# The down-projection of a hybrid decoder layer as seven block products: weight sums formed during FoX attention, zero blocks on ScalarE, low parts and additions on VectorE

## The chip, the cores and the metric

The kernel runs on one core of a Trainium2 chip. The metric is the device time of one execution in microseconds, the median of several runs. Engine names follow the profile: PE is TensorE (PEld its weight loads), DVE is VectorE, ACT is ScalarE, POOL is GpSimd, and SP is SyncE, which here only issues transfers.

## The reference

One decoder layer on 2048 tokens of width 1024, all in float32. The part that matters here:

```python
h = rms_norm(x, g_attn[l]) * (1.0 + scale_a) + shift_a
proj = h @ w_in[l]                      # FoX q|k|v, stick-breaking q|k|v, forget gates
o_fox = forgetting_attention(...)       # 8 heads of 64, causal softmax with a forget bias
o_sb = stick_breaking_attention(...)    # 8 heads of 64
x = x + gate_a * (mix @ w_out[l])

h = rms_norm(x, g_mlp[l]) * (1.0 + scale_m) + shift_m
u = causal_depthwise_conv(h @ w_up[l], conv_w[l], conv_b[l])
u_gate, u_val = jnp.split(u, 2, axis=-1)            # each 2752 wide
x = x + gate_m * ((jax.nn.silu(u_gate) * u_val) @ w_down[l])
return rms_norm(x, g_final)
```

`shift`, `scale` and `gate` come from a conditioning vector through `w_ada` (adaLN). The down-projection is the last product: 2048 tokens by 2752 by 1024.

## The kernel before

Every float32 operand of a matmul is split by `split` into a high part (a ScalarE copy, rounded to TensorE's fast float32 format) and a low part (the difference, by GpSimd unless VectorE is named). A product is then three matmuls: high by high, high by low, low by high.

The program has five stages: the stick-breaking heads with their input projections, the FoX heads with theirs, the output projection with the second norm, the up-projection with convolution and gating, and the down-projection with the final norm. In the attention stages a unit is a pair of heads and a block of 512 queries (4 pairs x 4 blocks for each kind). `interleave` runs a unit's attention and, in between, steps of generators: the projections of the next unit, and in FoX units the generator `late_mod` (4 steps a unit), which computes the rest of the adaLN modulation, folds `gate_a` into `w_out` (`fold_out`) and, at the end of its gate part, stores `gate_m` to device memory (line 565). Projection inputs and everything of `late_mod` live in one pool of ten tiles named `hp`. In `weighted`, a diagonal block's upper quarter of the tile `at` is zeroed by GpSimd (line 391) before ScalarE writes the rest. `Fd` (line 446) is the causal mask that GpSimd writes into the forget bias.

The up-projection already works as seven block products in place of eight (Winograd's form of Strassen's scheme): `h_operands` and `w_operands` form sums of quarter blocks, `pair` runs the products. It starts each half of the tokens with `h_operands`, whose tiles are `oa` and `ob`.

The down-projection runs plainly: for each of four blocks of 512 tokens, 22 row blocks of `w_down` (the last half full) are loaded and split each time, and eight banks of PSUM accumulate all of them. The last four row blocks are kept back so that the banks finish one after the other; then the gate, the residual `x1s`, the final norm and the store follow.

The program's code gives each engine a list of instructions in order; the scheduler of the framework places them by its own timeline, so that neighbouring stages overlap a little. Each engine works through its list in that order, and SP issues its transfers in that order too.

Of the kernel before, what the change touches and what calls it, by code (L numbers as in the profile page):

```python
# [33 lines left out]
def kernel(ctx: ExitStack, tc: tile.TileContext, x, c, w_ada, b_ada, g_attn, w_in, b_fgate,  # L34
# [28 lines left out]
    gate_m = dram.tile([P, D], F32, name="gate_m")  # L63
# [318 lines left out]
    def weighted(o, kts, blk, V, hl, first, last, diag):  # L382
# [7 lines left out]
        if diag:  # L390
            nc.gpsimd.memset(f(at[:, :, 0:P]), 0.0)
# [132 lines left out]

    def late_mod():
# [15 lines left out]
        for part, gate in late:  # L541
# [12 lines left out]
            if gate is not None:  # L554
# [7 lines left out]
                if gate == 0:  # L562
                    yield from fold_out(gt)
                else:
                    nc.sync.dma_start(gate_m, gt)
# [93 lines left out]
    for i, u in enumerate(units):  # L659
# [20 lines left out]
        if nxt is None:  # L680
# [10 lines left out]
                    (lm if kind == "fox" and (p, tb) != (0, 0) else None, 4, False), (tail, 12, True)])  # L691
# [44 lines left out]

    ho1 = open_pool("hop1")
# [12 lines left out]
    def h_operands(sblk, j):  # L750

        pool = ho if j == 0 else ho1
# [3 lines left out]
        b = pool.tile([P, 3, 2, TB], F32R, name=f"ob{j}")  # L756
        a = pool.tile([P, 4, 2, TB], F32R, name=f"oa{j}")
# [5 lines left out]
        def put(hi, lo, s, lo_engine=None):  # L763
            split(hi, lo, s, lo_engine or nc.vector)
# [8 lines left out]
        put(a[:, 1:3, 0], a[:, 1:3, 1], xh[:, 1].rearrange("p (a n) -> p a n", n=TB), nc.gpsimd)  # L773
# [150 lines left out]
    close_pool("up", "hop1", "wup", "hop0")  # L924

    dp = open_pool("down", side="right")

    def load(k, tb):
        n = P if k < NFULL else REST
        g = dp.tile([P, 2, TB], F32R, name="g", bufs=6)  # L930
        wraw = dp.tile([P, D], F32, name="wdraw", bufs=3)
        graw = dp.tile([P, TB], F32, name="graw", bufs=2)
        w = dp.tile([P, 2, D], F32R, name="wd", bufs=6)
        for r in range(P // n):
            nc.sync.dma_start(wraw[r * n:(r + 1) * n], w_down[k * P:k * P + n, :])
            nc.sync.dma_start(graw[r * n:(r + 1) * n], gs[k][tb // 2][:, tb % 2 * TB:(tb % 2 + 1) * TB])
        split(w[:, 0], w[:, 1], wraw, nc.vector)
        if n == P:
            split(g[:, 0], g[:, 1], graw)
        else:  # L940
            nc.scalar.activation(g[:, 0], graw, AF.Copy)
            nc.vector.tensor_sub(g[REST:P, 0], graw[REST:P], f(g[REST:P, 0]))
        return g, w

    de = open_pool("end")
    gm = de.tile([P, D], F32, name="gm")
# [3 lines left out]
    for tb in range(NTB):  # L950
# [13 lines left out]
        for k in range(NKD):  # L964
            g, w = load(k, tb)
            if k >= NKD - LAST:
                tail.append((k, g, w))
                continue
# [52 lines left out]
```

## Time and profile before

| | us |
|---|---|
| median of 3 runs (3137.22 to 3140.04) | 3139.62 |
| the profiled execution | 3137.58 |
| its span, first to last instruction | 3135.8 |
| TensorE busy | 2962.9 |
| VectorE busy | 2142.5 |
| ScalarE busy | 1650.2 |
| GpSimd busy | 1281.3 |

The page's busy times overlap, since the engines work side by side; a matmul's own duration also overlaps its neighbour's, so the pace of matmuls is taken from stretches of them. A row of a group reads: line, engine, operation, tile written, tiles read, shapes and count, then busy time and mean ns of one, then idle time before them and who ended it. A row of the waits reads: who waited, for whom, us in total, times, longest.

### The profile page before, as it was taken

To read this page: it belongs to the slowest core of one execution; us is meant where nothing else is said; L and a number is where in the kernel's file an instruction comes from. 1 tells how busy PE (TensorE), PEld (TensorE's weight loads), DVE (VectorE), ACT (ScalarE), POOL (GpSimd) and SP (SyncE) were. 2 spreads that over 40 slices of the span, in tenths; PEclk is the share of its full clock that TensorE was granted. 3 is DMA by queue.
4 is the path that set the end of the run, shared out by engine and by line. 5 is a ranking of instruction groups with operands and counts; after the bars stand their busy time and mean duration, and the time that the engine had idled before them with its cause. 6 is when DMAs were issued, how large, how long until landed. Compare 5 with 4: busy or idle time off the path is not lost. (4 is left out here: it accounts for less than half of the span.)

```text
span 3135.8 us, 46430 instructions
## 1 busy us (share of the span) xinstructions
PE 2962.9 (94%) x15934; PEld 2508.4 (80%) x15934; DVE 2142.5 (68%) x3334; ACT 1650.2 (53%) x3033; POOL 1281.3 (41%) x1523
## 2 busy tenths in 40 slices
PE   6889998999989999999999899999899998999998
PEld 5778787878878888888877688888678887888887
DVE  6787988888866765557832677778887776254253
ACT  5665666666656665567733444444444444333332
POOL 2564455456553343352212444444544442332321
PEclk8999999999999999999999999999999999999999
DMA  9447642556346796595456532223222223554552
GB/s 268 170 149 250 175 139 64 189 178 167 124 150 184 258 279 209 152 328 137 161 186 220 195 98 81 81 81 88 77 89 86 81 81 137 186 199 161 188 200 89
DMA packets 292940, 496.51 MB, mean 158 GB/s; under 512 B 29448, under 2 KB 177664, under 8 KB 291680
## 3 DMA queue, kind: packets, MB, share of 16 engines
q1 hardware_dynamic: 281072, 480.92, 48.0%
q10 hardware_dynamic: 11632, 12.63, 1.1%
q8 instruction: 126, 2.06, 0.3%
q14 instruction: 110, 0.90, 0.1%
HBM read 352.61 MB, written 90.51 MB: 141 GB/s over the span
## 5 line engine op out<-in xcount | busy, mean ns | idle before, releaser
L810 PE MATMUL ps_o<-oa,wu 128*128 128x512 f32 x2088 | 506.2, 393 | 18.1 <-DVE oa L45 12.0
L810 PEld LDWEIGHTS ps_o<-oa,wu 128*128 128x128 f32 x2088 | 392.4, 189 | 110.0 <-DVE oa L45 15.7
L397 PE MATMUL ps_pv<-at,V 128*128 128x256 f32 x2304 | 404.7, 294 | 36.2 <-DVE at L393 19.5
L393 DVE TENSOR_TENSOR at<-ps_pt,at 128x512 fp32r<-128x512 f32 (+1 forms) x576 | 364.0, 652 | 107.2 <-ACT at L392 104.2
L281 PE MATMUL ps_pj<-hp,w_qk 128*128 128x512 f32 x1512 | 415.2, 405 | 14.2 <-DMA hp<-hs 4.4
L392 ACT ACTIVATE at<-ps_pt 128x512 fp32r<-128x512 f32 (+1 forms) x576 | 314.4, 576 | 210.2 <-PE ps_pt L388 161.0
L420 POOL TENSOR_TENSOR a<-a,r 128x512 f32<-128x512 f32 (+3 forms) x240 | 286.8, 1196 | 309.8 <-DVE r L419 88.5
L397 PEld LDWEIGHTS ps_pv<-at,V 128*128 128x128 f32 x2304 | 334.6, 191 | 81.0 <-DVE at L393 34.5
L281 PEld LDWEIGHTS ps_pj<-hp,w_qk 128*128 128x128 f32 x1512 | 275.6, 191 | 68.7 <-DMA hp<-hs 6.9
L45 DVE TENSOR_TENSOR wd<-wdraw,wd 128x1024 fp32r<-128x1024 f32 x88 | 111.8, 1271 | 263.0 <-ACT wd L44 262.9
L45 POOL TENSOR_TENSOR g<-graw,g 128x512 fp32r<-128x512 f32 x84 | 142.3, 1696 | 326.5 <-ACT g L44 325.8
L378 PE MATMUL ps_qk<-K,Q 128*128 128x512 f32 (+2 forms) x640 | 265.7, 417 | 9.6 <-DMA K<-q 5.6
L419 DVE TENSOR_TENSOR_SCAN r<-r 128x513 f32<-128x513 f32 x192 | 258.9, 1360 | 19.4 <-ACT r L410 11.5
L960 PE MATMUL ps_o<-wd,g 128*128 128x512 f32 x1040 | 251.1, 391 | 8.7 <-ACT g L44 8.7
L810 PE MATMUL ps_t<-ob,wu 128*128 128x512 f32 x984 | 242.5, 391 | 0.3 <-ACT wu L44 0.3
L379 PE MATMUL ps_qk<-K,Q 128*128 128x512 f32 (+2 forms) x640 | 237.8, 373 | 0.0
L320 PE MATMUL ps_pj<-w_v,hp 128*128 128x256 f32 (+1 forms) x1536 | 230.8, 290 | 6.6 <-DVE q L290 2.9
L960 PEld LDWEIGHTS ps_o<-wd,g 128*128 128x128 f32 x1040 | 196.2, 189 | 50.0 <-ACT g L44 9.2
L44 ACT ACTIVATE wu<-wuraw 128x512 fp32r<-128x512 f32 x214 | 133.1, 626 | 184.2 <-PE ps_o L810 111.8
L320 PEld LDWEIGHTS ps_pj<-w_v,hp 128*128 128x128 f32 x1536 | 210.1, 193 | 16.5 <-DVE q L290 3.8
L810 PEld LDWEIGHTS ps_t<-ob,wu 128*128 128x128 f32 x984 | 185.3, 189 | 39.8 <-ACT wu L44 0.7
L44 ACT ACTIVATE wd<-wdraw 128x1024 fp32r<-128x1024 f32 x88 | 93.1, 1058 | 213.3 <-PE ps_bc L960 197.9
(218 smaller groups left out, 5834.1 us busy)
## 6 DMA issues: line engine op xcount, KB each, us to landing
hp<-hs SPq DMA_DIRECT2D x224, 512.0 KB
wuraw<-in_w_up_dram SPq DMA_DIRECT2D x84, 512.0 KB
wdraw<-in_w_down_dram SPq DMA_DIRECT2D x84, 512.0 KB
Q<-q SPq DMA_DIRECT2D x128, 256.0 KB
g<-u SPq DMA_DIRECT2D x42, 512.0 KB
graw<-g SPq DMA_DIRECT2D x84, 256.0 KB
hs<-hp SPq DMA_DIRECT2D x32, 512.0 KB
K<-q SPq DMA_DIRECT2D x128, 128.0 KB
```

The source lines that it names most:

```text
L45: (lo_engine or nc.gpsimd).tensor_sub(lo, src, f(hi))
L281: nc.tensor.matmul(acc, w[kt][:, a, n], h[:, bb], start=kt == 0 and i == 0, stop=kt == KT - 1 and i == 2)
L320: nc.tensor.matmul(av[:, t * width:(t + 1) * width], hts[kt][:, a, tok], w[1][kt][:, bb, 0:width], start=kt == 0 and m == 0, stop=kt == KT ...
L378: nc.tensor.matmul(b[:, :cw], Q[:, hl, 0, qcols], K[:, hl, :cw], start=True, stop=False)
L379: nc.tensor.matmul(b[:, :cw], Q[:, hl, 1, qcols], K[:, hl, :cw], start=False, stop=True)
L392: nc.scalar.activation(at[:, 0, lo:], b[:, lo:], AF.Copy)
L393: nc.vector.tensor_sub(at[:, 1, lo:], b[:, lo:], f(at[:, 0, lo:]))
L397: nc.tensor.matmul(o[:, 0:2 * P], V[kt // 4][:, kt % 4, hl, :], rhs, start=first and kk == 0 and w == 0, stop=last and kk == 1 and w == 1)
L419: nc.vector.tensor_tensor_scan(rev, rev, rev, 1.0, ALU.mult, ALU.bypass)
L420: (nc.vector if (ch + qi) % 4 == 0 else nc.gpsimd).tensor_mul(a[:, :need], a[:, :need], r[:, 1:need + 1])
L810: nc.tensor.matmul(b, w[:, p, j], o[:, q], start=first and i == 0, stop=last and i == 2, skip_group_check=True)
L960: nc.tensor.matmul(banks[t][n], g[:, a, t * P:(t + 1) * P], w[:, b, n * TB:(n + 1) * TB], start=k == 0 and i == 0, stop=k == NKD - 1 and i ...
```

## The change

Four parts.

1. **Weight sums in FoX.** The gate of the channel mixer is multiplied into `w_down`'s columns, and seven sums of its quarter blocks are formed once and stored to device memory. `fold_down` does this in `late_mod`, in 22 pieces (a pair of 128-row blocks, 512 of the 1024 columns): two loads and two products on GpSimd, four sums on GpSimd, seven stores on SP. `late_mod` gets 7 steps a unit instead of 4.
2. **The down-projection** becomes seven products of sums, over 11 pairs of row blocks (the missing half block is padded with zeros) in three chunks of 3, 4 and 4 pairs, and for each chunk over eight pairs of 128-token blocks. All seven weight sums of a chunk stay in SBUF, split once. The residual `x1s` is loaded, added to and stored again in every chunk; in the last one the final norm follows. Low parts and all additions are VectorE's, but for two weight sums whose low part is GpSimd's.
3. **Zero blocks**: the upper quarter of `at` is written by a ScalarE copy from a block of zeros.
4. **`h_operands`**: a low part goes from GpSimd to VectorE, and the `ob` tiles of the later blocks get a pool of their own.

```diff
@@ weighted
         if diag:
-            nc.gpsimd.memset(f(at[:, :, 0:P]), 0.0)
+            nc.scalar.activation(at[:, :, 0:P], edge[:, 0:2 * P].rearrange("p (a n) -> p a n", n=P), AF.Copy)
@@ new, called by late_mod in place of the store of gate_m
+    def fold_down(gt):
+        q4 = lambda x: x.rearrange("p (h q n) -> p q h n", h=2, n=2 * P)
+        for m, q in ((m, q) for m in range(NM) for q in range(2)):
+            t = wide().rearrange("p (w n) -> p w n", n=2 * P)
...
+            for i, rows_ in ((0, P), (1, n)):
+                row = (2 * m + i) * P
+                nc.sync.dma_start(t[0:rows_, 2 * i:2 * i + 2], q4(w_down[row:row + rows_, :])[:, q])
+                nc.gpsimd.tensor_mul(t[:, 2 * i:2 * i + 2], t[:, 2 * i:2 * i + 2], q4(gt)[:, q])
+            yield
+            a1, a2, b1, b2 = (t[:, i] for i in range(4))
...
+            for o, x in ((0, a1), (2, b1), (5, b2)):
+                nc.sync.dma_start(to[o], x)
+            nc.gpsimd.tensor_sub(b2, b2, a2)
+            nc.gpsimd.tensor_sub(a2, a2, a1)
+            nc.gpsimd.tensor_add(a1, b2, a1)
+            nc.gpsimd.tensor_sub(b1, b1, a1)
+            for o, x in ((4, b2), (3, a2), (1, a1), (6, b1)):
+                nc.sync.dma_start(to[o], x)
+            yield
@@ the units' loop
-                    (lm if kind == "fox" and (p, tb) != (0, 0) else None, 4, False), (tail, 12, True)])
+                    (lm if kind == "fox" and (p, tb) != (0, 0) else None, 7, False), (tail, 12, True)])
@@ h_operands
-        put(a[:, 1:3, 0], a[:, 1:3, 1], xh[:, 1].rearrange("p (a n) -> p a n", n=TB), nc.gpsimd)
+        put(a[:, 1:3, 0], a[:, 1:3, 1], xh[:, 1].rearrange("p (a n) -> p a n", n=TB))
@@ the down-projection, in place of the plain one
+    def down_operand(c, o):
+        n = CHUNKS[c][1]
+        w = dw.tile([P, 2, 4, TB], F32R, name="wb", bufs=7)
+        raw = wr.tile([P, 4, TB], F32, name="wbraw", bufs=3)
+        nc.sync.dma_start(raw[:, 0:n], wds[c][o])
+        split(w[:, 0, 0:n], w[:, 1, 0:n], raw[:, 0:n], nc.gpsimd if o in (3, 5) else nc.vector)
+        return w
+    def g_operands(c, tp):
...
+        nc.gpsimd.tensor_sub(s3, a11, a21)
+        nc.gpsimd.tensor_add(a21, a21, a22)
+        nc.gpsimd.tensor_sub(s2, a21, a11)
+        yield put(a11)
+        yield put(s2)
+        yield put(a12)
+        nc.gpsimd.tensor_sub(a12, a12, s2)
...
+        def run(b, o, first, last):
+            for m in range(n):
+                for k, (p, q) in enumerate(((0, 0), (0, 1), (1, 0))):
+                    nc.tensor.matmul(b, ga[o][:, p, m], wbs[o][:, q, m], start=first and m == 0 and k == 0,
+                                     stop=last and m == n - 1 and k == 2, skip_group_check=True)
+            if nxt is not None:
+                later.append(next(nxt))
+            if turn:
+                wlater.append(down_operand(c + 1, o))
...
+        nc.scalar.activation(p1, a, AF.Copy)
+        for t, half in ((1, L), (1, H), (0, H)):
+            nc.vector.tensor_add(xs[t][:, half], xs[t][:, half], p1)
+        b = bank_a()
+        run(b, 1, True, True)
+        take(1, L, b)
+        run(a, 2, False, True)
+        take(0, L, a)
+        square(0, L)
+        run(b, 3, False, True)
+        take(1, H, b)
...
```

Here `take` adds a bank to the residual tile `xo`, and `put` splits a sum of gated values into the tile `ga` (8 buffers, VectorE's low part).

Where it moves instructions: first SP's queue in FoX. Before, where the gate is stored (`hp` from `hs` are projection inputs, `K` and `Q` the next unit's keys and queries, `wd` with two numbers the stored weight sums):

```order
L293 DMA Q_16641<-q2_16644 64x1024 x4
L256 DMA raw_qk_17123<-in_w_in_dram 128x2x128
L256 DMA raw_qk_17128<-in_w_in_dram 128x2x128
L303 DMA K_16642<-q2_16645 64x512 x4
L545 DMA hp_16592<-in_w_ada_dram 128x1024
L565 DMA gate_m_234<-hp_16258 128x1024
L509 DMA os2_1_101<-oT_15868 128x512
```

And now, SP in the same part of FoX:

```order
L348 DMA hp_14980<-hs0_6_66 128x1024
L550 DMA wd6_0_240<-hp_14899 128x256
L348 DMA hp_14985<-hs0_7_67 128x1024
L537 DMA hp_15128<-in_w_down_dram 128x2x256 x2
L511 DMA os1_2_98<-oT_14090 128x512
L544 DMA wd0_0_234<-hp_15128 128x256
L544 DMA wd2_0_236<-hp_15128 128x256
L544 DMA wd5_0_239<-hp_15128 128x256
L305 DMA K_15069<-q2_15072 64x512
L295 DMA Q_15068<-q2_15071 64x1024 x4
L550 DMA wd4_0_238<-hp_15128 128x256
L550 DMA wd3_0_237<-hp_15128 128x256
```

The one store has become seven a piece, and projection inputs, keys and queries of the next unit stand between them and behind them.

GpSimd's queue in FoX before, with the masks, the modulation's sums (line 552) and a zero block:

```order
L446 AFFINE_SELECT Fd_16727<-Fb_15451 128x384
L552 TENSOR_TENSOR hp_16591<-hp_16591,hp_16760 128x512
L391 MEMSET at_16544 128x2x128
L552 TENSOR_TENSOR hp_16591<-hp_16591,hp_16760 128x512
L446 AFFINE_SELECT Fd_16748<-Fb_15451 128x512
```

GpSimd's queue in FoX now, at the first four pieces:

```order
L45 TENSOR_TENSOR w_v_14726<-raw_v_14724,w_v_14726 128x256
L538 TENSOR_TENSOR hp_14280<-hp_14280,hp_14125 128x512 x2
L538 TENSOR_TENSOR hp_14461<-hp_14461,hp_14125 128x512 x2
L538 TENSOR_TENSOR hp_14624<-hp_14624,hp_14125 128x512 x2
L538 TENSOR_TENSOR hp_14899<-hp_14899,hp_14125 128x512 x2
L45 TENSOR_TENSOR w_v_14731<-raw_v_14729,w_v_14731 128x256
L45 TENSOR_TENSOR w_v_14736<-raw_v_14734,w_v_14736 128x256
L448 AFFINE_SELECT Fd_14413<-Fb_13303 128x512
L45 TENSOR_TENSOR w_v_14741<-raw_v_14739,w_v_14741 128x256
L545 TENSOR_TENSOR hp_14280<-hp_14280 128x256
```

The zero blocks are gone from it, and products and sums of the pieces stand ahead of masks and of the low parts of the next heads' weights.

ScalarE's queue at the start of the down-projection before; `g` and `wd` are its operands, the SiLU above them (line 921) is the up-projection's last:

```order
L876 ACTIVATE u_28137<-y_28081,conv_254 128x1024
L921 ACTIVATE u_28141<-u_28137 64x1024
L44 ACTIVATE wd_28170<-wdraw_28168 128x1024
L44 ACTIVATE g_28167<-graw_28169 128x512
L44 ACTIVATE wd_28204<-wdraw_28202 128x1024
```

And now, where `wb` are weight sums and `ga` sums of gated values:

```order
L904 ACTIVATE u_28513<-y_28457,conv_274 128x1024
L949 ACTIVATE u_28517<-u_28513 64x1024
L44 ACTIVATE ga_28560<-graw_28548 128x384
L44 ACTIVATE ga_28568<-gsum_28555 128x384
L44 ACTIVATE ga_28576<-graw_28548 128x384
L44 ACTIVATE ga_28585<-graw_28548 128x384
L44 ACTIVATE ga_28593<-gsum_28556 128x384
L44 ACTIVATE ga_28601<-graw_28548 128x384
L44 ACTIVATE ga_28609<-graw_28548 128x384
L44 ACTIVATE ga_28638<-graw_28626 128x384
L44 ACTIVATE wb_28543<-wbraw_28544 128x1536
L44 ACTIVATE wb_28563<-wbraw_28564 128x1536
```

Eight narrow high parts now stand between the SiLU and the first weight part that a matmul can use.

More of the change, by code (lines that the diff above doesn't have):

```diff
@@ L923 @@
         nc.sync.dma_start(gs[NFULL][sblk], sg[REST:P])
[L924 to L943, printed above, removed]
+    close_pool("up", "hop1", "hopb1", "wup", "hop0")
```

142 lines of the change are left out of this document (92 added, 50 removed).

## The prediction

> **What bounds the kernel now.** I read the page's totals first, then the busy time by stage, then the chain that ended last, then the waits of TensorE.
>
> ```profile
> span 3135.8 us, 46430 instructions
> PE 2962.9 (94%) x15934; PEld 2508.4 (80%) x15934; DVE 2142.5 (68%) x3334; ACT 1650.2 (53%) x3033; POOL 1281.3 (41%) x1523
> ```
>
> Next, the stages: us, then busy time and count of PE, PEld, DVE, ACT, POOL, then clock, DMA share and GB/s. The rows are stick-breaking, FoX, up-projection, and two stretches of the down-projection.
>
> ```profile
> 70.00:912.00 842.00, 771.08 (x4910) 674.49 (x4911) 697.08 (x961) 548.91 (x1185) 460.32 (x693) 0.97 0.48 153
> 912.00:1565.00 653.00, 635.45 (x4192) 566.65 (x4192) 436.90 (x1129) 413.06 (x766) 227.61 (x342) 0.99 0.68 218
> 1790.00:2651.00 861.00, 832.89 (x3601) 677.29 (x3600) 678.15 (x756) 383.39 (x541) 372.29 (x308) 0.99 0.28 84
> 2900.00:3018.00 118.00, 118.00 (x522) 97.69 (x522) 48.48 (x56) 41.31 (x64) 35.63 (x22) 1.00 0.54 184
> 3018.00:3136.00 118.00, 109.79 (x485) 90.58 (x483) 41.55 (x54) 33.20 (x54) 26.59 (x17) 0.98 0.40 135
> ```
>
> TensorE is busy for all 118 us of a down-projection block while VectorE works 48 us, so matmuls alone set that stage's length. The groups by line count them, and one step of the chain gives their pace.
>
> ```profile
> L960 PE MATMUL ps_o<-wd,g 128*128 128x512 f32 x1040 | 251.1, 391 | 8.7 <-ACT g L44 8.7
> L960 PE MATMUL ps_t<-wd,g 128*128 128x512 f32 x520 | 131.7, 391 | 0.0
> L960 PE MATMUL ps_bc<-wd,g 128*128 128x512 f32 x520 | 131.7, 390 | 0.0
> 2872.11 9.97 PE ps_o L960 x44
> ```
>
> The means of 391 ns overlap; 44 in 9.97 us is 0.2266 us each, and 2080 of them are 471 us of the 483 us from 2653.12 to the end. The rest is a slow first stretch and the tail.
>
> **The matmuls.** The new stage has 7 products, 11 row pairs, 3 terms and 8 token pairs: 7 x 11 x 3 x 8 = 1848. That is 232 fewer, not an eighth, because the half-filled last row block is padded and gets its third term. 232 x 0.2266 = **-52.6 us**, the one sure term.
>
> **Start of the stage.** The handover today, first TensorE, then ScalarE:
>
> ```profile
> 2636.75 7.64 PE L810 MATMUL ps_o<-oa,wu 128*128 128x512 f32 x33
> 2653.12 2.07 PE L960 MATMUL ps_o<-wd,g 128*128 128x512 f32 x4 [8.73 <-ACT g L44]
> 2649.17 1.05 ACT L921 ACTIVATE u<-u 64x1024 f32<-64x1024 f32 x1 [2.73 <-DVE u L879]
> 2651.49 1.06 ACT L44 ACTIVATE wd<-wdraw 128x1024 fp32r<-128x1024 f32 x1 [1.26 <-DMA wdraw<-in_w_down_dram]
> ```
>
> The new ScalarE queue puts eight 384-wide high parts and a 1536-wide weight part behind that SiLU, which ends at 2650.2. Prices:
>
> ```profile
> L392 ACT ACTIVATE at<-ps_pt 128x384 fp32r<-128x384 f32 x128 | 63.0, 493 | 27.0 <-PE ps_pt L388 22.9 <-PE ps_pv L397 2.8 <-issue 0.3
> L44 ACT ACTIVATE wd<-wdraw 128x1024 fp32r<-128x1024 f32 x88 | 93.1, 1058 | 213.3 <-PE ps_bc L960 197.9 <-DMA wdraw<-in_w_down_dram 15.3
> L452 ACT ACTIVATE p<-p,mn 128x2048 f32<-128x2048 f32 x8 | 16.0, 2002 | 3.0 <-DVE mn L448 3.0
> L45 DVE TENSOR_TENSOR wd<-wdraw,wd 128x1024 fp32r<-128x1024 f32 x88 | 111.8, 1271 | 263.0 <-ACT wd L44 262.9
> ```
>
> 8 x 0.493 + 1.53 (between 1058 and 2002 ns) gives 2655.7; VectorE's low part, 1.5 x 1.27 = 1.9, gives 2657.6 against 2653.12: 4.5 us later. The later weight sums queue behind three raw buffers and about 2.5 MB of residual and gain loads; the first two token pairs interleave on TensorE, which covers most. I take **+6** (0 if the queue fills early, +14 if GpSimd's two low parts are late too).
>
> **The two changes of weight chunk.** Seven sums of 2048 columns must be split while the last pair of the old chunk and the first of the new run: 63 + 84 matmuls, 33.3 us, at the first change; 168, 38.1 us, at the second. ScalarE needs 7 x 2.0 + 14 x 0.62 + 2 x 0.6 = 24 us: it fits. VectorE's price rows:
>
> ```profile
> L45 DVE TENSOR_TENSOR wu<-wuraw,wu 128x512 fp32r<-128x512 f32 x214 | 177.9, 834 | 20.0 <-ACT wu L44 20.0
> L864 DVE TENSOR_TENSOR y<-ps_o,snap 128x512 f32<-128x512 f32 x40 | 27.4, 686 | 11.3 <-PE ps_o L810 9.2
> L984 DVE TENSOR_TENSOR xo<-xo,yo 128x512 f32<-128x512 f32 x32 | 25.7, 803 | 0.6
> L992 DVE SCALAR_TENSOR_TENSOR xo<-xo,r_f,gf 128x512 f32<-128x512 f32 x32 | 26.6, 871 | 0.3
> ```
>
> A token pair costs 7 x 0.83 + 3 x 0.80 + 6 x 0.69 = 12.4 us, plus 4 x 0.87 in the last chunk, 15.9, of TensorE's 19.0: the steady state stays with TensorE. A pair of the narrow first chunk costs 10.9 (low parts at 0.62). A change adds 5 x 2.54 = 12.7, so 36 against 33.3 and 41 against 38.1; about a pair's operands are ready ahead, which absorbs most. I take **+3 each, +6** (0 to +23, rival C).
>
> **Steady state and tail.** TensorE now waits for additions out of PSUM, as the up-projection does; there that wait is small:
>
> ```profile
> PE ps_o L810 <- DVE snap L859: 1.1, 4, 0.4
> ```
>
> The last product is followed by the same addition, square, root, scaling and store; dropping the gate multiply (0.69) pays for the first row's scaling still ahead in the queue. **+2** (0 to +10). ScalarE does 7 x 0.62 + 0.6 + 4 x 0.8 = 8 us of a pair's 19. The transfers stay hidden: a pair loads 1 MB of gated values and loads and stores 1 MB of residual each way, 3 MB in 19 us or 158 GB/s, where the stage moves 184 now; a change of chunk adds 7 MB over some 38 us, 184 more, close to the 330 of the FoX stretch below, and is part of the upper bound there.
>
> **FoX.** The 22 pieces of `fold_down` (a pair of 128-row blocks, half of the columns) come here, and the late modulation runs at 7 steps a unit (a head pair's block of 512 queries) instead of 4. Each piece has two 128x512 products and four 128x256 sums on GpSimd, 2 loads and 7 stores on SP.
>
> ```profile
> L552 POOL TENSOR_TENSOR hp<-hp 128x512 f32<-128x512 f32 x56 | 71.3, 1289 | 62.2 <-ACT hp L551 57.9 <-issue 4.2
> L614 POOL TENSOR_TENSOR o<-o,r 128x256 f32<-128x256 f32 x64 | 47.7, 747 | 116.3 <-DMA r<-rstd 87.6 <-DMA o<-os 12.7 <-DVE x L633 6.3
> L522 SPq DMA_DIRECT2D wos<-hp x16: 519/558/912, 1035.3 to 1168.3; - x16
> 1080.00:1130.00 50.00, 49.53 (x308) 42.66 (x307) 38.69 (x101) 34.89 (x73) 24.26 (x38) 1.00 0.95 330
> PE ps_pj L281 <- DMA hp<-hs: 4.4, 4, 1.5
> POOL Fd L446 <- DVE mn L448: 133.5, 72, 6.7
> ```
>
> GpSimd: 22 x (2 x 1.29 + 4 x 0.75) = 123 us onto 228 of 653. SP: 198 issues of up to 0.56 us are 110 us. DMA: 11 MB read and 20 MB written, over 44/7 = 6.3 units of about 41 us, 31 MB / 257 us = 121 GB/s above some 170. In 1080 to 1130 the transfers ran at 330 GB/s and TensorE was still busy 49.53 of 50 us, and its waits for projection inputs were 4.4 us over FoX: the cover is real. What loses it is order. A later sum overwrites what an earlier store reads, so GpSimd waits for stores; SP stands in front of stores until GpSimd has computed; and the next unit's projection inputs, Q and K stand behind those on SP. Masks (Fd) stand behind the sums on GpSimd, though today they wait 133.5 us for VectorE, so they have room. Bounds: -2 (quicker modulation ends early) to +45 (2 us of stall for each piece). I take 0.55 us a piece, **+12**, nearer the covered end since the rows above show cover.
>
> **Zero blocks.** 128 memsets leave GpSimd, 128 copies come to ScalarE:
>
> ```profile
> L391 POOL MEMSET at<- 128x256 f32 x128 | 39.5, 311 | 171.8 <-PE ps_pv L397 160.4 <-PE ps_pt L388 3.9 <-DVE at L393 3.8
> L44 ACT ACTIVATE mix<-o 128x256 fp32r<-128x256 f32 x64 | 26.3, 415 | 71.4 <-POOL o L614 62.8 <-DMA hm<-hf_m 8.1 <-ACT hf_m L715 0.4
> PE ps_pt L388 <- POOL a L420: 10.8, 14, 1.9
> ```
>
> GpSimd loses 40 us of work and 172 us of standing in its queue for the buffer; ScalarE gains 128 x 0.415 = 53 us, half of it in stick-breaking, where it is busy 549 of 842 us. What is queued behind the copy on ScalarE is the high part of the same tile, which needs the same buffer and the transposes besides, so the wait is no new one. TensorE's waits for GpSimd's products there are 10.8 us: **-2** (-10 to +6).
>
> **Up-projection.** Eight low parts go from GpSimd to VectorE.
>
> ```profile
> L45 POOL TENSOR_TENSOR oa<-xh,oa 128x1024 fp32r<-128x1024 f32 x8 | 25.2, 3151 | 4.2 <-ACT oa L44 4.2
> L45 DVE TENSOR_TENSOR oa<-xh,oa 128x512 fp32r<-128x512 f32 x16 | 25.2, 1594 | 2.7 <-ACT oa L44 2.7
> PE ps_o L810 <- DVE oa L45: 10.5, 5, 4.2
> 1798.07 1.75 DVE L768 TENSOR_TENSOR tt<-xh 128x512 f32<-128x512 f32 x1 [2.50 <-POOL xh L767]
> 1797.99 1.27 POOL L796 TENSOR_TENSOR ws<-wuraw 128x512 f32<-128x512 f32 x1
> ```
>
> VectorE gains 8 x 1.27 = 10 us, but its neighbours that take 1594 ns beside GpSimd come nearer to 834. TensorE waits 10.5 us there: **-4** (-8 to +3).
>
> **Sum.** -52.6 + 6 + 6 + 2 + 12 - 2 - 4 = -32.6. The profiled execution took 3137.58 (span 3135.8 and 1.8 around it), giving 3105.0; the median of the runs, 3139.62, lies 2.0 higher, so **3107**.
>
> In the last two rows above a VectorE operation with both inputs in SBUF took 1.75 us beside a GpSimd one of 1.27. The Trainium skill (SBUF — State Buffer, "Who interferes with whom") says that the two share a read port which one holds for its whole instruction. The rows agree with it; rival C is what that exclusion would do here.
>
> **Rivals.**
> A, the forecast: 3085 to 3126 as its own range; chance 0.60.
> B, FoX gives it back: GpSimd and SP serialize `fold_down`, at about 1.9 us a piece +42 instead of +12, 3137. For it: nothing in FoX has slack on TensorE (635 of 653). Against: the 330 GB/s stretch. 0.13.
> C, the exclusion binds at the chunk changes: VectorE's two-SBUF-input work is 12.7 + 14 x 0.69 + 6 x 0.69 = 26.5, GpSimd's two 2048-wide low parts and eight subtractions 2 x 2 x 2.4 + 8 x 1.29 = 19.9 (2.4 for 1024, twice 1.29, below the 3151 seen beside VectorE). Their sum 46.4 exceeds 33.3 by 13 and, with 3.5 more for the scaling, 38.1 by 12: +25 instead of +6, 3126. Against: work ready ahead. 0.10.
> D, slower: if each piece holds SP, and with it the next unit's inputs, for its whole GpSimd time of 5.6 us, FoX grows by 22 x 5.6 = 123 less the cover; half of it uncovered is 62 instead of 12, 3157. It decides from (32.6 + 12) / 22 = 2.0 us a piece. 0.11.
> E, more gain: no stall at the changes, none in FoX, and GpSimd's freed queue worth 10: 3081. 0.06.
>
> A change of 0.2%, 6 us, is about the least that these runs can tell from none. Faster: A, C, E and nearly half of B, 0.82; same, the rest of B, 0.07; slower, D, 0.11. The range holds A, C, E's upper half and B: 3080 to 3141.
>
> **What would show it.** Right: 1848 down matmuls at 0.227 us, the first near 2658 less what stages before gain, and under 10 us of TensorE idle around each chunk change; FoX's stage 5 to 20 us longer. Wrong: FoX with TensorE waiting for projection inputs or Q and K by tens of us (B, D), or waits of TensorE for VectorE's weight low parts at the changes (C).

## The result and the profile after

The changed kernel took 3170.99 us (median of 4 runs, 3167.53 to 3171.73) beside 3139.83 (3137.22 to 3144.87) for the kernel before on the same chip: a ratio of 1.0091, 95% interval 1.0079 to 1.0104. It is 31 us slower; the forecast was 33 faster. The profiled executions have spans of 3169.7 and 3135.8 us, 33.9 apart.

The page's first lines, after:

```profile
span 3169.7 us, 46978 instructions
PE 2941.7 (93%) x15702; PEld 2487.3 (78%) x15702; DVE 2327.3 (73%) x3585; ACT 1692.3 (53%) x3198; POOL 1377.0 (43%) x1547
```

TensorE has 232 instructions fewer and is busy 21 us less, in a span that is 34 longer.

Two events mark the stages in every kernel here: the first full mask product of FoX on VectorE (tile `p` from `ps_qk` and `Fb`) and the last store of an attention result (`os` from `oT`). A row of the timeline by tile gives shortest, middle and longest duration in ns, then first and last start. Before, then after:

```profile
L448 DVE CUSTOM_DVE_ANT_0 p<-ps_qk,Fb x96: 629/685/693, 927.0 to 1559.6; 128x512 f32<-128x512 f32 x96
L509 SPq DMA_DIRECT2D os<-oT x32: 319/335/542, 113.3 to 1588.6; - x32
```

```profile
L450 DVE CUSTOM_DVE_ANT_0 p<-ps_qk,Fb x96: 670/686/695, 939.3 to 1617.5; 128x512 f32<-128x512 f32 x96
L511 SPq DMA_DIRECT2D os<-oT x32: 319/338/1082, 113.6 to 1648.9; - x32
```

With the start of the last matmul of the up-projection (2644 and 2700) as a third mark, the difference splits so:

| stage | before | after | change | forecast |
|---|---|---|---|---|
| stick-breaking, to the first mask product | 927.0 | 939.3 | +12.3 | -2 (all of the zero blocks) |
| FoX, to the last `os` store | 661.6 | 709.6 | +48.0 | +12 |
| output projection and up-projection | 1055.4 | 1051.2 | -4.2 | -4 |
| down-projection, to the end | 491.8 | 469.6 | -22.2 | -38.6 |

The stages again, as in the prediction: stick-breaking, FoX, up-projection, and two stretches of the down-projection away from its chunk changes, the second in the last chunk.

```profile
70.00:918.00 848.00, 768.26 (x4861) 669.59 (x4862) 698.65 (x958) 566.38 (x1248) 445.15 (x631) 0.97 0.48 152
918.00:1625.00 707.00, 655.03 (x4222) 582.06 (x4221) 447.92 (x1128) 434.25 (x826) 322.43 (x410) 0.97 0.75 244
1852.00:2699.00 847.00, 829.08 (x3597) 674.36 (x3596) 671.40 (x758) 382.48 (x540) 364.17 (x303) 0.99 0.27 83
2860.00:2995.00 135.00, 134.56 (x593) 110.78 (x592) 97.60 (x121) 42.29 (x62) 51.20 (x35) 1.00 0.60 203
3020.00:3150.00 130.00, 127.23 (x559) 104.41 (x558) 107.27 (x161) 52.64 (x120) 35.96 (x29) 1.00 0.41 141
```

In the fourth row 593 matmuls take 134.56 us, 0.2269 each: the steady state of the new stage is TensorE's. FoX holds the loss. Between its own two marks, before and after:

```profile
927.00:1588.60 661.60, 643.54 (x4216) 572.49 (x4216) 440.85 (x1125) 414.56 (x760) 220.35 (x333) 0.99 0.66 212
```

```profile
939.30:1648.90 709.60, 657.63 (x4214) 582.98 (x4213) 449.96 (x1121) 432.68 (x818) 321.50 (x404) 0.97 0.75 242
```

With almost the same matmuls TensorE stands 52 us instead of 18 and is busy 14 us longer, at a granted clock of 0.97 instead of 0.99. So 34 of the 48 us are standing, and 14 are the same matmuls at a lower clock: between these marks the trace records half clock for 41.0 us, and for 6.8 us before.

**In FoX**, the waits of TensorE, then of SP, then of GpSimd on the fold's own lines:

```profile
PE ps_pj L283 <- DMA hp<-hs: 28.2, 12, 4.1
SPq L544 <- POOL hp L538: 29.9, 24, 3.2
SPq L537 <- DMA wd<-hp: 18.8, 6, 4.4
SPq L550 <- POOL hp L545: 13.6, 10, 2.4
POOL hp L538 <- DMA hp<-in_w_down_dram: 59.7, 18, 7.9
POOL hp L545 <- DMA wd<-hp: 40.3, 15, 9.1
```

TensorE waits 28.2 us for projection inputs (4.4 before). SP stands 43.5 us in front of stores for GpSimd's products and sums, and 18.8 in front of a load for a buffer whose stores have not landed; GpSimd stands 59.7 for loads and 40.3 for stores. One such place on SP's queue, then TensorE:

```profile
1339.59 2.76 SPq L550 DMA_DIRECT2D wd<-hp  x4
1345.50 1.26 SPq L537 DMA_DIRECT2D hp<-in_w_down_dram  x2
1346.86 1.02 SPq L348 DMA_DIRECT2D hp<-hs  x2
1352.76 2.32 SPq L348 DMA_DIRECT2D hp<-hs  x4
1352.75 5.49 PE L283 MATMUL ps_pj<-hp,w_qk 128*128 128x512 f32 x12 [4.07 <-DMA hp<-hs]
```

SP has issued four stores of a piece by 1342.35. It then stands 3.0 us until stores from the tile that it fills next have landed, issues two loads of pieces, and only then, at 1346.86, sends two projection inputs. TensorE waits 4.07 us for the first of these two (the next four leave as the wait ends), and its 12 matmuls then take 5.49 us instead of 12 x 0.2266 = 2.7: the granted clock is 0.50 over these 5.49 us.

**At the start of the down-projection**, TensorE, SP and ScalarE:

```profile
2716.54 0.79 PE L1022 MATMUL ps_o<-wb,ga 128*128 128x512 f32 x1 [16.03 <-ACT wb L44]
2700.12 0.37 SPq L966 DMA_DIRECT2D wbraw<-wd  x1
2700.67 3.07 SPq L980 DMA_DIRECT2D graw<-g  x6
2705.30 1.05 ACT L949 ACTIVATE u<-u 64x1024 f32<-64x1024 f32 x1 [2.73 <-DVE u L907]
2707.28 0.52 ACT L44 ACTIVATE ga<-graw 128x384 fp32r<-128x384 f32 x1 [0.93 <-DMA graw<-g]
2710.83 0.52 ACT L44 ACTIVATE ga<-gsum 128x384 fp32r<-128x384 f32 x1 [3.03 <-POOL gsum L992]
2713.77 1.35 ACT L44 ACTIVATE ga<-graw 128x384 fp32r<-128x384 f32 x3 [1.17 <-POOL graw L996]
2715.02 4.21 ACT L44 ACTIVATE wb<-wbraw 128x1536 fp32r<-128x1536 f32 x3
```

The first loads leave at 2700.12, as the up-projection's matmuls end, not ahead of it, and the first weight part starts on ScalarE at 2715.02. The wait is 16.03 us where it was 8.73. The up-projection's SiLU ends 5.8 us after TensorE's last matmul, as before, at 2706.35. The eight gated parts then take ScalarE 8.7 us, because it stands 3.03 and 1.17 us for GpSimd's sums and 0.93 for a load between them.

**At a change of chunk**, the timeline's rows of TensorE, VectorE and GpSimd, and then a window over TensorE's row (us, busy and count of PE, granted clock, DMA share, GB/s):

```profile
2849.97 4.38 PE L1022 MATMUL ps_o<-wb,ga 128*128 128x512 f32 x11 [2.83 <-DVE xo L1030]
2842.54 5.10 DVE L45 TENSOR_TENSOR ga<-graw,ga 128x512 fp32r<-128x512 f32 x1
2840.79 6.31 POOL L45 TENSOR_TENSOR wb<-wbraw,wb 128x2048 fp32r<-128x2048 f32 x1 [0.32 <-ACT wb L44]
```

```profile
2849.97:2854.35 4.38, 4.38 (x12) 0.61 1.01 421
```

A 128x512 low part, 0.83 us on the average in the up-projection before, takes 5.10 on VectorE and ends, at 2847.6, 0.5 us after GpSimd's piece of 6.31. The addition that frees TensorE's bank stands behind it.

### The profile page after: what moved, and what is told of

Same layout as the page of the kernel before. It is cut to its first block, busy times and chain, and to the rows that moved or that the text cites. A ratio compares the mean times of both kernels' runs of the same rounds, so it can differ in the third digit from the quotient of the medians.

```text
span 3169.7 us, 46978 instructions
## 1 busy us (share of the span) xinstructions
PE 2941.7 (93%) x15702; PEld 2487.3 (78%) x15702; DVE 2327.3 (73%) x3585; ACT 1692.3 (53%) x3198; POOL 1377.0 (43%) x1547
## 5 line engine op out<-in xcount | busy, mean ns | idle before, releaser
L283 PE MATMUL ps_pj<-hp,w_qk 128*128 128x512 f32 x1512 | 426.0, 412 | 35.7 <-DMA hp<-hs 28.2
L399 PE MATMUL ps_pv<-at,V 128*128 128x256 f32 x2304 | 413.2, 297 | 39.9 <-DVE at L395 26.6
L1022 PE MATMUL ps_o<-wb,ga 128*128 128x512 f32 x1320 | 319.9, 398 | 28.8 <-ACT wb L44 16.6
L1022 PEld LDWEIGHTS ps_o<-wb,ga 128*128 128x128 f32 x1320 | 253.0, 192 | 86.7 <-ACT wb L44 17.5
L390 PE MATMUL ps_pt<-edge,a 128*128 128x128 f32 x1088 | 187.1, 281 | 28.2 <-POOL a L422 13.6
L412 ACT ACTIVATE r<-ps_qk 128x512 f32<-128x512 f32 (+2 forms) x320 | 173.0, 541 | 51.0 <-PE ps_qk L381 46.4
L45 DVE TENSOR_TENSOR wu<-wuraw,wu 128x512 fp32r<-128x512 f32 x214 | 180.0, 844 | 22.3 <-ACT wu L44 22.2
```

The costliest lines, as they stand in the source:

```text
L283: nc.tensor.matmul(acc, w[kt][:, a, n], h[:, bb], start=kt == 0 and i == 0, stop=kt == KT - 1 and i == 2)
L390: nc.tensor.transpose(b[:, i * P:(i + 1) * P], blk(kts[kk], qi), ident)
L399: nc.tensor.matmul(o[:, 0:2 * P], V[kt // 4][:, kt % 4, hl, :], rhs, start=first and kk == 0 and w == 0, stop=last and kk == 1 and w == 1)
L1022: nc.tensor.matmul(b, ga[o][:, p, m], wbs[o][:, q, m], start=first and m == 0 and k == 0, stop=last and m == n - 1 and k == 2, skip_group_ ...
```

## The experiments

In what follows the fold is `fold_down` with its place in `late_mod`. Most kernels of the first group are the kernel before with the fold added and its own down-projection kept, so that they show FoX alone. FoX's length is that between the two marks. The kernel before was timed beside each group of runs, with medians of 3143.6 to 3147.8 us, so kernels of different groups are compared by their ratios.

### The fold in FoX

**The fold alone** (`f_fold`: kernel before, `late_mod` at 7 steps, `yield from fold_down(gt)` after the store of `gate_m`).

> Kernel before plus fold_down at 7 steps a unit; the old down-projection stays and the sums are stored but not used. All theories that put the loss in FoX: that stage 50 to 60 us longer than before, about 3193. If the loss came from other parts of the change (zero blocks, the new order of the whole program): under 20 us longer.

**Seven steps without the fold** (`f_rate7`: only `4, False` to `7, False`).

> Kernel before with late_mod at 7 steps a unit and no fold_down. Theory 'the pieces are the load': within 6 us of before, 3134 to 3146. Rival 'the quicker modulation and fold_out crowd the transfers': 15 to 25 us slower, since units (0,2) to (1,0) of FoX alone lost about 20 us in the changed kernel, before the first piece.

**Without the stores** (`f_nostore`: `f_fold` less its two loops of `nc.sync.dma_start(to[o], x)`), and **stores issued by GpSimd** (`f_gq`: in them `nc.sync` to `nc.gpsimd`).

> f_fold without the stores of the sums (left out: 20 MB of writes and 154 issues; loads and GpSimd's work stay). SP order or saturated transfers: most of the loss goes, 3145 to 3160. Rival 'hp buffers are short, or GpSimd's sums delay masks': over 3175.

> f_fold with the pieces' stores issued by GpSimd itself instead of SP. Theory 'SP stands in front of stores that wait for GpSimd, and projection inputs stand behind it': TensorE's waits for projection inputs fall from about 28 to under 10 us and most of the loss goes, 3150 to 3165. Rival 'hp buffers are short' or 'transfers are saturated': no change from f_fold, over 3180.

**Transfers without arithmetic** (`f_dma`: `f_fold` less products and sums) and **arithmetic without transfers** (`f_pool`: `f_fold` less loads and stores; `tensor_mul(t[...], q4(gt)[:, q], q4(gt)[:, q])`).

> The kernel before with the fold in FoX at seven steps a unit, its loads and its seven stores a piece, but without GpSimd's products and sums (the stores write w_down as it was loaded, and nothing reads them). Whole fold: 3195 us beside 3143; seven steps alone: 3155; fold without stores: 3174. Theory transfers (the fold's 44 loads and 154 stores, and the buffers that they hold, delay h): 3175 to 3200 us. Rival GpSimd (its products and sums stand in order ahead of FoX's own work, and the stores wait for them): 3153 to 3167 us, near the seven steps alone.

> The kernel before with the fold's products and sums on GpSimd at seven steps a unit, but none of its loads and stores (the products read the gate twice, and nothing is written out). Theory transfers: 3152 to 3163 us, as seven steps alone (3155). Rival GpSimd: 3172 to 3198 us.

**Fewer stores** (`f_merge`, with the seven sums side by side in device memory) and **products and sums on VectorE** (`f_dve`: `nc.gpsimd` to `nc.vector` on five lines).

```diff
-            for o, x in ((0, a1), (2, b1), (5, b2)):
-                nc.sync.dma_start(to[o], x)
+            nc.sync.dma_start(to[:, 0], a1)
+            nc.sync.dma_start(to[:, 1:3], t[:, 2:4])
...
-            for o, x in ((4, b2), (3, a2), (1, a1), (6, b1)):
-                nc.sync.dma_start(to[o], x)
+            nc.sync.dma_start(to[:, 3:7], t)
```

> The kernel before with the fold in FoX at seven steps a unit, its seven stores a piece written as three transfers (the planes lie side by side in device memory), 66 in place of 154. The fold as it was: some 51 us over before; without stores: 30. Theory A (the number of stores: SP issues in order, and each one stands in front of h): 28 to 42 us over before. Theory B (the bytes of the stores and the buffers that they hold until they land): 44 to 58 over.

> The kernel before with the fold in FoX at seven steps a unit, its products and sums on VectorE in place of GpSimd. Transfers without arithmetic lie 28 us over before, the arithmetic alone on GpSimd 18, the seven steps alone 10 to 12, all together 51. Theory A (GpSimd's pieces are slow, wait in order for loads, and hold the buffers): 26 to 40 us over before. Theory B (any engine that takes the pieces in order stops for their loads; VectorE is on FoX's path): 50 to 90 over.

Measured, with the ratio to before (and its interval), FoX's length in the profile (661.6 before), and TensorE's wait for `hp` from `hs` between 912 and 1645 us (4.4 before):

| kernel | ratio | FoX | wait |
|---|---|---|---|
| f_rate7 | 1.0031 (1.0015 to 1.0047) | 673.0 | 9.2 |
| f_pool | 1.0057 (1.0034 to 1.0079) | 678.6 | 12.4 |
| f_dma | 1.0088 (1.0066 to 1.0109) | 697.8 | 18.8 |
| f_nostore | 1.0100 (1.0071 to 1.0130) | 691.3 | 10.3 |
| f_merge | 1.0112 (1.0096 to 1.0129) | 698.6 | 22.4 |
| f_dve | 1.0166 (1.0142 to 1.0191) | 713.9 | 18.2 |
| f_fold | 1.0168 (1.0139 to 1.0198) | 711.6 | 35.5 |
| f_gq | 1.0331 (1.0301 to 1.0361) | 768.8 | 38.2 |

The fold alone gives FoX +50.0, as the changed kernel has (+48.0): the loss of FoX is the fold's and needs nothing else of the change. Of it, 11 us is the faster modulation, which the prediction gave no price of its own (its lower bound had it as a gain of 2). Its place is seen in one window of the two profiles, before and with seven steps:

```profile
1000.00:1100.00 100.00, 98.60 (x641) 86.41 (x640) 80.86 (x206) 67.60 (x123) 28.01 (x49) 1.00 0.69 228
```

```profile
1000.00:1100.00 100.00, 87.91 (x540) 76.35 (x539) 69.99 (x170) 60.57 (x108) 36.15 (x48) 0.97 0.91 301
```

Without any fold, the columns of the modulation and the rows of `w_out` come at 301 GB/s instead of 228, and TensorE does 540 matmuls in place of 641 there; part of that is won back later, since 101 matmuls are some 16 us at that pace and the whole is 11.

Above the seven steps, GpSimd's arithmetic alone adds 6 us of FoX, transfers alone 25, loads and arithmetic 18, all of it 39. Each length is from one profile; the 6 us are not told from none, since the intervals of `f_pool` and `f_rate7` overlap. No one part holds the loss: the seven steps, the fold without stores and the transfers alone all fell between what the theories expected; only the arithmetic alone fell where the theory of the transfers had it. Three transfers for seven, with the same bytes, give 1.0112 for 1.0168, intervals apart, and FoX is 13 us shorter, so bytes alone do not make the price. The merged stores also wait for other sums than the single ones did, so their number and their order are not told apart. VectorE in GpSimd's place changes nothing on balance (1.0166): TensorE waits 18.2 us for inputs instead of 35.5, but has new waits behind VectorE, `ps_pv` for `at` 9.1 us. How much of the fold's price GpSimd's pace makes, that swap does not tell.

The stores on GpSimd's queue were to free SP. They cost 51 us more. The groups of that kernel between 1100 and 1660 us, then two waits of SP between 1100 and 1500 us:

```profile
L552 POOL DMA_DIRECT2D wd<-hp x88 | 49.3, 560 | 0.5 <-POOL at L395 0.5
L546 POOL DMA_DIRECT2D wd<-hp x66 | 36.8, 560 | 1.0 <-issue 0.7 <-POOL Fd L450 0.2
```

```profile
SPq L539 <- DMA wd<-hp: 34.6, 6, 20.1
SPq L350 <- DMA wd<-hp: 24.8, 5, 18.3
```

Each issue holds GpSimd 560 ns, 86 us in all, in a queue on which FoX's masks stand. And SP, though free of the stores, now stands 59.4 us in front of loads for tiles of `hp` whose stores have not landed (13.6 and 5.4 in `f_fold`). So TensorE's wait for inputs stays, 38.2 us. A clean test of SP's order it was not: it took another engine's time and held the tiles longer. That the ten tiles of `hp`, more than the order of the stores on SP, keep the inputs waiting is a rival that stays open.

**Two buffers for all pieces** (`f_two`: `t = ring[(2 * m + q) % 2]`, where `ring` is two tiles of the pool `hp` taken once).

> The kernel before with the weight sums added in FoX at seven steps a unit (old second stage kept), but the seven sums' pieces alternate between two tiles that are taken from the ten hp buffers once, instead of taking a new buffer for each of the 22 pieces. The same fold with a buffer for each piece took 3195 us beside 3143 for before. Theory hp (the pieces hold too many of the ten buffers, so that the loads of h for the projections start late): 3150 to 3175 us, and TensorE's waits on hp<-hs in FoX fall from 35.5 us to under 15. Rival DMA (the fold's own transfers crowd those of h in the queues): 3185 to 3205 us, waits on hp<-hs unchanged.

The profiled run took 3278.9 us, far from either theory; the second, 3464.4, is left out, since its granted clock was 0.886 beside 0.963. TensorE stands once for almost the whole fold (its waits between 1200 and 1380 us):

```profile
PE ps_pj L285 <- DMA hp<-hs: 99.2, 4, 96.3
```

The input that ends this wait leaves SP at 1341.0, when the pieces are nearly through. We read it so: the pool hands its ten tiles out in turn, and an input that is due the tile of a held piece waits for it. No other run shows this, and it is no measure of the shortage in the fold as written.

**The modulation and the fold from stick-breaking on** (`f_spread`: `lm if i >= 8 and (kind, p, tb) != ("fox", 0, 0) else None, 5`).

> The kernel before with the weight sums, whose late modulation and folds run from the third head pair of stick-breaking on (units 8 and later) at five steps a unit, instead of in FoX alone at seven. Theory DMA (too much transferred per unit in FoX): 3143 to 3168 us, TensorE's waits on hp<-hs in FoX under 12 us, and the stretch from 1000 to 1100 us is no longer above a DMA share of 0.85. Rival hp or order (each piece costs a fixed delay wherever it stands): 3180 to 3200 us, the loss of some 50 us only moved, part of it into stick-breaking. A third way: VectorE, 84% busy in stick-breaking, takes the split of fold_out's rows there badly: stick-breaking grows by over 15 us.

It gave 1.0236 (1.0221 to 1.0252). FoX is 691.7 us long, +30, and the first mask product stands at 976.3, 49 later, as the third way of the expectation has it. Only 21 of the 154 stores leave before that mark, so the pieces can hardly be what lengthened stick-breaking: the modulation and `fold_out` came there with them, and FoX kept most of the pieces. Whether the pieces would be cheaper in stick-breaking this run does not say.

### Zero blocks

**Zero blocks by ScalarE alone** (`z_act`, part 3 of the change on the kernel before), and **back on GpSimd in the changed kernel** (`a_zg`).

> The kernel before with only the zero blocks written by ScalarE instead of GpSimd. Theory (the zero copy stands ahead of ScalarE's and VectorE's work on the same tile on the path of the diagonal units, and explains the 6 us that stick-breaking lost): 3146 to 3152 us, stick-breaking 5 to 8 us longer in the profile. Rival (the 6 us came from elsewhere in the changed kernel, or from the throttle): within 3 us of before, stick-breaking 842 us as before.

> The changed kernel with the zero blocks on GpSimd again and nothing else. Alone, on the kernel before, the zero blocks on ScalarE cost 12 to 15 us. Theory (that price stands in the changed kernel too): 3155 to 3163 us beside 3143 for before, the first mask product of FoX 10 us earlier in the profile. Rival (in FoX the crowded GpSimd is glad of the blocks it lost, and the fold's loss grows by as much): 3168 to 3180 us.

Alone it costs 1.0039 (1.0026 to 1.0052), some 12 us, with the first mask product at 942.3. Over all profiles here that mark stands at 933.1 to 942.3 in the three kernels with ScalarE's zeros and at 923.4 to 931.2 in the sixteen others that start FoX like the kernel before (`f_spread` left out). So the sign of that term was wrong. The group of the copies in stick-breaking (70 to 912 us) of `z_act`:

```profile
L391 ACT ACTIVATE at<-edge 128x256 fp32r<-128x256 f32 x62 | 26.2, 422 | 7.0 <-PE ps_pv L397 7.0
```

It is 26.2 us of work, as priced, with 7.0 of standing for the buffer. TensorE's wait for `at` from VectorE (line 393) rises from 18.8 to 24.2 us there, and for GpSimd's products (line 420) from 10.8 to 14.3. ScalarE is 67% busy in that stage (563.8 of 842 us). Both waits are on the path from scores to weights, and the copies now stand on ScalarE ahead of the same tile's high part, where GpSimd's memsets had stood beside it; the two rises are 9 us of the 15 by which the mark is later.

Taken back in the changed kernel, the price does not show: 1.0084 (1.0064 to 1.0104) against 1.0091. The mark is early (923.4), but FoX is 718.6 long, 9 more. This is the rival's picture, though one profile against a spread of some 9 us in the marks does not settle it.

### The second stage

**GpSimd's two weight parts in four pieces, and pools in another order** (`d_both`, the changed kernel with both):

```diff
+        if o in (3, 5):
+            nc.scalar.activation(w[:, 0, 0:n], raw[:, 0:n], AF.Copy)
+            for m in range(n):
+                nc.gpsimd.tensor_sub(w[:, 1, m], raw[:, m], f(w[:, 0, m]))
...
-    ga_ = open_pool("dga", side="right")
-    wr = open_pool("dwr", side="right")
     dg = open_pool("dg", side="right")
+    ga_ = open_pool("dga", side="right")
+    wr = open_pool("dwr", side="right")
```

> The changed kernel (3171 us) with GpSimd's low parts of the weight sums in four pieces of 128x512 instead of one of 128x2048, and with the pools of the second stage opened in another order, so that the first gated rows' tiles take the space that comes free first. Theory (the start of the stage, 16.0 us of wait, and the two chunk changes, each a VectorE piece of 5.1 us held up beside a GpSimd piece of 5 to 6.3 us, cost some 20 us over the sum): 3152 to 3163 us; the largest wait of TensorE at the start falls under 11 us and no piece of VectorE of 128x512 takes over 2.5 us at a chunk change. Rival (the clock gate or the next wait takes it back): 3166 to 3174 us.

1.0079 (1.0057 to 1.0101): no change that can be told. The windows around the two changes of chunk and the stretch between them, of the changed kernel, then of this one:

```profile
2842.00:2860.00 18.00, 15.17 (x59) 0.91 0.81 303
2860.00:2995.00 135.00, 134.56 (x593) 1.00 0.60 203
2995.00:3020.00 25.00, 22.14 (x92) 0.93 0.68 244
```

```profile
2837.00:2855.00 18.00, 16.58 (x72) 1.00 0.97 342
2855.00:2990.00 135.00, 130.62 (x564) 0.97 0.57 193
2990.00:3015.00 25.00, 24.16 (x107) 1.00 0.77 270
```

The changes do 28 matmuls more in the same 43 us, 6 us, and no VectorE piece of 128x512 takes over 1.8 us around the first one. The long stretch between does 29 fewer. So the blocked piece was a cause of the pauses, and most of what its removal won was given back: in the long stretch TensorE waits 3.4 us for an addition and 0.9 for a gated low part, where it waited 0.4. The first wait of the stage stays, 16.7 us: the first load leaves 2.0 us ahead of the end of the up-projection's matmuls instead of 0.4, and ScalarE still does eight gated parts ahead of a weight part.

### Another place for the fold

**In the up-projection, in a ring of its own** (`u_fold`: four steps a unit again, zeros on GpSimd, 44 half-width pieces called twice, at some column blocks three times), **the same with the edits of `d_both`** (`u_best`), and **in the ring of the tiles `snap`**, six instead of four (`u_pace`, also with them).

> The changed kernel with the fold taken out of FoX (late modulation at four steps a unit again) and put into the up-projection, in 44 pieces of half the width in a small pool of their own, and with the zero blocks on GpSimd again. Theory (the second stage is worth 29.5 us, the up-projection 4, and the loss of the changed kernel is that of FoX and of the zero blocks; the up-projection has DMA at 0.26 and GpSimd at 0.44): 3106 to 3124 us beside 3143 for before. Rival (the fold costs 1 to 2.5 us a piece wherever it stands, by GpSimd's pieces holding up VectorE, which is 78% busy there): 3130 to 3165 us, with TensorE under 97% busy in the up-projection.

> The same, with GpSimd's low parts of the weight sums in four pieces and with the other order of the second stage's pools. Theory: 2 to 8 us under the kernel that only moves the fold, 3102 to 3118 us. Rival: no difference to it.

> The changed kernel with the fold in the up-projection, one piece of half the width for each column block: the piece's tile is taken in turn from the ring of the tiles snap, so that the scheduler can't draw all pieces to the stage's start, as it did where the fold had a ring of its own (44 pieces between 1800 and 2180 us, 3207 us). Zero blocks on GpSimd, GpSimd's low parts in four pieces, the other order of pools. Theory (the fold is cheap where each piece finds GpSimd and the queues free): 3104 to 3128 us beside 3143 to 3148 for before, TensorE over 98% busy from 1900 to 2250 us. Rival (the pieces hold up the up-projection's own weight sums on GpSimd, in order, wherever they stand): 3140 to 3200 us, TensorE under 95% busy in that stretch.

They gave 1.0200 (1.0180 to 1.0220), 1.0167 (1.0142 to 1.0191) and 1.0124 (1.0105 to 1.0143). FoX is cured in all three: the last `os` store stands at 1595.5, 1585.7 and 1591.0. From there to the up-projection's last matmul it is now 1135, 1134 and 1118 us instead of 1055. In `u_fold` the scheduler drew all pieces into 1800 to 2200 us; tied to `snap` they spread over the stage. A window of `u_fold`, then one of `u_pace` and the same of before:

```profile
1900.00:2000.00 100.00, 84.23 (x325) 65.22 (x324) 63.61 (x67) 31.72 (x47) 88.22 (x109) 0.90 0.54 152
```

```profile
1900.00:2200.00 300.00, 281.04 (x1204) 225.57 (x1205) 229.54 (x246) 120.80 (x173) 176.12 (x194) 0.99 0.39 114
```

```profile
1900.00:2200.00 300.00, 299.10 (x1312) 245.01 (x1311) 236.27 (x267) 133.64 (x190) 125.95 (x126) 1.00 0.27 83
```

Even spread, the stage does 1204 matmuls where it did 1312. The time and TensorE's busy share, 94%, are what the rival expected; its mechanism is not shown. GpSimd is busy 59% of these 300 us and stands 20.6 in front of a sum for its store. But ScalarE waits 56.2 us behind GpSimd's line of `y` and 49.1 for its weight sums, together no more than before, 70.5 and 37.5. TensorE's own waits there are for VectorE (`snap` 12.4 us, `y` 6.9), and why these grew is open. A free share on an engine did not make the work free.

### What the runs pointed to

**Fold on VectorE, three stores a piece, zeros on GpSimd, the edits of `d_both`** (`c_all`), and **one step a piece at 5.5 steps a unit** (`c_slow`).

> The changed kernel with what the runs point to: fold on VectorE, three stores a piece, zero blocks on GpSimd, GpSimd's low parts in the second stage in four pieces, the other order of its pools. If A holds for both: FoX 22 to 35 us over before instead of 54, stick-breaking as before, second stage and up-projection 36 to 40 under: 3130 to 3145 us beside 3143 to 3146. If not: 3155 to 3200.

> The same with one step a piece instead of two and 5.5 steps a unit instead of seven: the modulation's columns then load at 5.5 a unit and the fold's pieces stand as close as at eleven half steps. Theory (seven steps alone cost 10 to 12 us, by columns that load faster than the queues carry them): 4 to 9 us under the kernel with seven. Rival (the pieces are the costly part, and they stand closer now): 5 to 25 us over it.

1.0056 (1.0039 to 1.0073) and 1.0064 (1.0046 to 1.0082). The first is some 11 us quicker than the changed kernel, intervals apart, and still slower than before; the slower rate makes no difference that can be told. In the profile of `c_all` the mark is early (930.2) and FoX 712.5: merged stores, worth 13 us of FoX beside GpSimd's sums, show nothing beside VectorE's. Why is open. No kernel here beats the one before.

## Why the prediction was wrong

**The matmuls** were right: 1320 and 528 in the groups of the new stage, 1848, and 0.2269 us each where nothing interferes.

```profile
L1022 PE MATMUL ps_o<-wb,ga 128*128 128x512 f32 x1320 | 319.9, 398 | 28.8 <-ACT wb L44 16.6 <-DVE xo L1030 11.5 <-DVE wb L45 0.6
L1022 PE MATMUL ps_t<-wb,ga 128*128 128x512 f32 x528 | 129.5, 389 | 1.0 <-ACT wb L44 1.0
```

**FoX** is the step that failed: +12 forecast, +48 measured. That is 2.2 us a piece, past the 2.0 from which rival D decides, or 1.7 without the seven steps, for the forecast 0.55. "The cover is real" was read from the stretch that moved 330 GB/s with TensorE busy. That stretch shows that TensorE can stay busy beside that many bytes when the transfers stand in the order that they had there. It says nothing of a queue in which stores wait for sums and sums for stores, ahead of inputs; the prediction named that order and then sized it by the bytes. Rival D had the mechanism (SP stands, inputs stand behind), and TensorE's waits for inputs bear out a part of it: 28.2 us instead of 4.4. 11 us of the 48 are the seven steps alone, which the prediction had put at nothing or a gain. Split the other way, 34 us are standing and 14 the lower clock behind it, which no term priced. `f_fold` shows that the fold with its seven steps is the whole of FoX's loss. Whether it comes by SP standing for GpSimd or by tiles of `hp` held until their stores land, the runs do not separate.

**Stick-breaking** was +12.3 for the -2 of the zero blocks. "The wait is no new one" was nearly so (7.0 us); what failed is that 26 us of work on ScalarE was thought free. `z_act` shows the price alone, 12 us of time. That ScalarE stands on the path there is argued from two waits of TensorE, and taking the copies back in the changed kernel did not bring the price back.

**The second stage** had its terms mis-sized, +16 in all, with the mechanisms named. At 0.2266 us a matmul, the windows give what each stretch lost:

```profile
2653.10:2670.00 16.90, 16.88 (x62) 0.82 0.88 343
```

```profile
2716.50:2740.00 23.50, 18.60 (x62) 0.79 0.76 280
3150.00:3169.70 19.70, 11.61 (x52) 0.86 0.27 100
```

The first 62 matmuls took 23.5 us (16.9 before), after a wait 7.3 longer: +14 for the forecast +6. The wait's term had the eight gated parts at 8 x 0.493 = 3.9 us; they took 8.7, since it left out that ScalarE stands for GpSimd's sums between them. In the stretch itself TensorE stands another 4.9 us, 2.74 of them at once for an addition of VectorE's, which no term had. The two changes lost 4.6 and 4.2 (18 less 59 x 0.2266, and 25 less 92 x 0.2266), +9 for +6: rival C's exclusion did bind, at a smaller price than C's +25. The tail loses 7.9, as before; the steady stretches another 5.5, with +2 forecast for both. With -52.6 these make -24 beside the -22.2 of the marks.

At the chunk change the row of VectorE, blocked 5.10 us beside GpSimd's 6.31, has two inputs in SBUF, and the GpSimd operation reads SBUF. The Trainium skill (SBUF — State Buffer, "Who interferes with whom") states that two such operations contend, and the trace agrees with it.

**The up-projection** was right: -4.2 for -4.

The terms that missed are FoX by 36, the second stage by 16 and stick-breaking by 14: 66, which is the way from a gain of 33 to a loss of 33 in the profile. The time, 3171, lies 30 above the range's end, because the range gave FoX +45 or the second stage its worst, but not three misses of one sign.

## What to carry to other kernels

Price work that is put beside a full engine by the queues it passes through, not by bytes or busy shares: 22 pieces with nine transfers each cost 39 us above the faster modulation, seven stores merged into three took 13 of that back beside GpSimd's sums, and the same sums in half-width pieces cost 62 to 80 us in a stage with DMA at 0.27 and GpSimd at 42%. Count a wait of TensorE for more than its length, since the clock falls behind it. A row that shows a transfer rate being tolerated is evidence for the order in which those transfers stood, and not for another order. Before shortening a stage at the end by work in an earlier one, run that work alone: `f_fold` shows the whole loss without any of the new second stage.

## What the hardware showed

A short wait costs TensorE more than its length. After 2.83 us of waiting at the chunk change the granted clock was 0.61 over the next 4.38 us, in which 12 matmuls ran instead of 19; after 4.07 us in FoX it was 0.50 over 5.49 us. The Trainium skill (TensorE: Matmul & The Clock Gate, "What's actually happening") says that the clock halves after an idle window of about 3.4 us and returns after as much activity. The trace agrees in kind: its clock records hold 1.0 and 0.5 alone, and in FoX each stretch of 0.5 lasts 3.41 us or twice that. But here it does not take 3.4 us of standing: a wait of 2.12 us that ended at 1054.50 was followed by half clock from 1054.65 to 1058.06.

A transfer issued by GpSimd held it 560 ns (154 of them, 86 us); in the same kernel an issue of the loads and stores of FoX's `hp` tiles on SP took 0.33 to 0.60 us in the middle, by kind, on an engine that only issues transfers.
